# Output projection: the second half of the contraction by Strassen's scheme too

## The chip, the cores and the metric

The kernel runs on one core of a Trainium2 chip. The metric is device time in microseconds of one execution, the median of several runs. Engines: TensorE (PE; PEld is its weight load), VectorE (DVE), ScalarE (ACT), GpSimd (POOL) and SyncE (SP), which here only issues DMAs.

## The reference, cut to what matters

One inference step of an encoder layer for two request groups that share all weights: 256 prompt rows and 32 sample rows, model width 1024. All branch inputs come from one combined projection of x. Branch A is an mLSTM matrix memory with 4 heads of 256, branch B a sparse attention with 8 heads of 128. The end of the layer, where the change lies:

```python
branch_a = (hn * sigmoid(oa)) * silu(za)
branch_b = o_b * silu(zb)
mixed = sigmoid(ga) * (branch_a @ w_out_a) + sigmoid(gb) * (branch_b @ w_out_b)
y = layer_norm(DN_ALPHA * x + mixed @ w_o, ln_g, ln_b)   # w_o: 1024 x 1024
```

Beside y, the outputs are the new keys and values, the indexer keys, and the mLSTM states C, n and m of both groups.

## The kernel before, in words

**Precision.** All large products are made in three parts. An fp32 operand v is split into a high part (a copy to the rounded type fp32r, by ScalarE) and a low part (v minus the high part, by VectorE); the product is high x high + high x low + low x high. So each weight tile of 128 x 1024 costs one ScalarE pass (`unit_hi`, `split_hi`), one VectorE operation (`unit_lo`, `split_lo`) and three matmuls for each 128 x 128 block.

**Main loop.** `ORDER` lists 117 weight tiles; all but the last eight (the tiles of w_o) are steps of the main loop, a tile each, 24 matmuls of 288 columns in some 3.2 us. `load_plan` gives each tile a step at which its load is issued on SP's queue and one of eight staging buffers. From step `EARLY + 4` on only four of the eight buffers rotate; the other four hold the first four tiles of w_o. In step t, in this order: the loads, the low part of tile t+2, the evacuation of tile t-1, the high part of tile t+3, and the 24 matmuls of tile t, with the work listed for the step by `at` or `start` (`side`) in the middle of them. High and low parts lie in rings of four buffers each (`pair`). Each engine works strictly in the order in which its instructions are written.

**mixed.** The last 16 steps are the tiles of the gate ga and of w_out_a in turn. The evacuation of each w_out_a tile (L1012 to L1015) multiplies, adds onto branch B's part in `mB`, copies the sample columns and splits the result into `mxh`, `mxl`. `mixed` therefore stands with its features on the partitions, 8 blocks of 128 features.

**Output projection** (`finish`, L1159). The first 512 features are a 2 x 2 block product of token halves (128 rows) and halves of columns (512) done by Strassen's scheme in Winograd's form: seven products (`seventh`, L1079, of 6 matmuls of 512 columns each) in place of eight. It needs sums of token blocks s1 to s4 (`token_sums`, `token_halves`, one operation for all low parts, L1030) and differences of weight blocks t1 to t4 (`weight_sum`), made by VectorE during the main loop. The second 512 features are done plainly: four calls of `plain` (L1085), each of 4 x 3 matmuls. The four blocks of y lie in four PSUM banks y11, y12, y21, y22; VectorE adds them onto alpha * x, the residual, half a row at a time (`begun`, L1165; `added`, L1169). The bank y21 also serves as running total, from which VectorE reads between products. The sample rows are one plain product of 64 small matmuls (`sample_rows`, L1098).

**Layer norm.** For each block of 128 rows VectorE records statistics (L1172), aggregates them (`statistics`, L1151), GpSimd raises the variance to the power -0.5 (L1156), VectorE centres and multiplies by g (L1176), then scales and adds b (L1181). Row block 0 is finished while TensorE still works on row block 1. Row block 1's last half is written by the second DMA of L1185.

**States.** `state_prompt(h)` (L776) makes one head's C_prompt: 12 matmuls of 258 columns, two copies by ScalarE (L789), and DMAs (SP for heads 0 and 1, ScalarE's queue for 2 and 3). All four heads stand at the very end, behind the matmuls of y; head 3's copies and DMAs are written last.

Of the kernel before, what the change touches and what calls it, by code (L numbers as in the profile page):

```python
# [19 lines left out]
D = 1024  # L20
# [11 lines left out]
SEVEN = ("b11", "b21", "t2", "t1", "t3")  # L32
# [53 lines left out]
EARLY = WO - 20  # L86


def load_plan():
    slots, homes = defaultdict(list), {}  # L90
    for t in range(FIRST, EARLY + 9):
        slots[max(t - 9, FIRST)].append(t)
        homes[t] = (t - FIRST) % 8
    for i in range(4):
        slots[EARLY + i].append(WO + i)
        homes[WO + i] = (EARLY + 9 + i - FIRST) % 8
    rest = [*range(EARLY + 9, WO), *range(WO + 4, NT)]
# [14 lines left out]
def body(ctx, tc, a, o):  # L112
# [37 lines left out]
    def load_tile(t):  # L150
        if t >= NT or t in loaded:
            return
        loaded.add(t)
        stage[t] = sb(f"wst{t}", [128, KT * 128], tag=f"wst{HOMES[t]}")
        sp.dma_start(stage[t], a["w"][:, t - FIRST])
# [5 lines left out]
    def raw_unit(u):  # L161
        if u[0] == "t":
            return lazy["sums"][u]
        if u[0] == "b":
            return stage[POS["wo", ("b11", "b12", "b21", "b22").index(u)]]
        return stage[POS["wo", int(u[1])]]
# [7 lines left out]
    def unit_lo(u):  # L174
        wh, wl = split[u]
        dve.tensor_tensor(wl, raw_unit(u), wh.bitcast(F32), OP.subtract)

# [839 lines left out]
    def token_sums():  # L1017
        m = lazy["mB"]
        a11, a12 = m[:, 0:2, 0:128], m[:, 2:4, 0:128]
        a21, a22 = m[:, 0:2, 128:256], m[:, 2:4, 128:256]  # L1020
        s1, s2, s3, s4 = (lazy["sraw"][:, i].rearrange("p (k t) -> p k t", k=2) for i in range(4))
# [5 lines left out]
    def token_halves():  # L1027
        both = sb("sums", [128, 2, 4, 256], F32R, tag="kaT")
        act.copy(both[:, 0], lazy["sraw"])
        dve.tensor_tensor(both[:, 1], lazy["sraw"], both[:, 0].bitcast(F32), OP.subtract)  # L1030
        for i in range(4):
            lazy["s", i + 1] = tuple(both[:, e, i].rearrange("p (k t) -> p k t", k=2) for e in range(2))

    def weight_sum(name):
        if "sums" not in lazy:
            t = sb("t123", [128, 3, KT * 128], tag="a5")
            lazy["sums"] = {"t1": t[:, 0], "t2": t[:, 1], "t3": t[:, 2], "t4": sb("t4", [128, KT * 128], tag="wmat")}
        first, second = {"t1": ("b12", "b11"), "t2": ("b22", "t1"), "t3": ("b22", "b12"), "t4": ("b21", "t2")}[name]
        dve.tensor_tensor(lazy["sums"][name], raw_unit(first), raw_unit(second), OP.subtract)

    at(WO - 6, token_sums)
    at(WO - 4, token_halves)
    for i, n in enumerate(("t1", "t2", "t3", "t4")):
        at(EARLY + 5 + 2 * i, weight_sum, n)
# [34 lines left out]
    def seventh(p, x, u, first=False):  # L1079
        x = standing(x)  # L1080
# [4 lines left out]
    def plain(p, rows, column, first=False):  # L1085
        r = slice(128 * rows, 128 * rows + 128)
        for k in range(4, KT):
            group(p, (lazy["mxh"][:, k, r], lazy["mxl"][:, k, r]), split[f"w{k}"],
                  slice(512 * column, 512 * column + 512), first and k == 4, k == KT - 1)

    def sample_rows(p):
        for k in range(KT):
            for q in range(4):
                if k < 4:
                    w, c = stage[POS["wo", 2 * (k // 2) + q // 2]], 512 * (k % 2) + 256 * (q % 2)
                else:
                    w, c = stage[POS["wo", k]], 256 * q
# [33 lines left out]
    def load_tail():  # L1131
        lazy["xn"] = sb("xn", [128, 2, D], tag="vaT")
        sq = sb("sq", [128, 8, 256], tag="stC")
        lazy["zs"], lazy["gs"], lazy["bs"], lazy["xs"] = (sq[:, i] for i in range(4))
        lazy["sraw"] = sq[:, 4:8]
        lazy["bst"] = sb("bst", [128, 2, 2, 6], tag="sg", bufs=3)
        lazy["bss"] = sb("bss", [128, 4, 6])
        sp.dma_start(lazy["xn"], a["x_nat"][0:TP].rearrange("(b p) c -> p b c", p=128))
        sp.dma_start(lazy["xs"], ap_of(a["x_nat"], TP * D, [[256, 4], [D, TS], [1, 256]]))

    def load_affine():
        gb = sb("rest", [128, 2, D], tag="xhl")
        lazy["g"], lazy["b"] = gb[:, 0], gb[:, 1]
        sp.dma_start(gb, ap_of(a["ln_gb"], 0, [[0, 128], [D, 2], [1, D]]))
# [14 lines left out]
    def finish():  # L1159
        z, zs, bst, bss = lazy["xn"], lazy["zs"], lazy["bst"], lazy["bss"]  # L1160
        g, be = lazy["g"], lazy["b"]

        def begun(b, c, p):
            half = slice(512 * c, 512 * c + 512)
            dve.scalar_tensor_tensor(z[:, b, half], z[:, b, half], ALPHA, p, op0=OP.mult, op1=OP.add)  # L1165

        def added(b, c, p):
            half = slice(512 * c, 512 * c + 512)
            dve.tensor_tensor(z[:, b, half], z[:, b, half], p, OP.add)  # L1169

        def recorded(b, c):
            dve.bn_stats(bst[:, b, c], z[:, b, 512 * c:512 * c + 512])  # L1172

        def centred(b):
            mv, nr = statistics(b, slice(0, 128), bst[:, b].rearrange("p a b -> p (a b)"))
            dve.scalar_tensor_tensor(z[:, b], z[:, b], mv[:, 0:1], g, op0=OP.subtract, op1=OP.mult)  # L1176
            return nr[:, 1:2]

        def scaled(b, rs):
            for c in (slice(0, 512), slice(512, 1024)):  # L1180
                dve.scalar_tensor_tensor(z[:, b, c], z[:, b, c], rs, be[:, c], op0=OP.mult, op1=OP.add)  # L1181

        def put(c):
            c = slice(512 * c, 512 * c + 512)
            sp.dma_start(o["y"][128:256, c], z[:, 1, c])  # L1185

        own = sb("wown", [128, 2, KT * 128], F32R, tag="a1")
        spare = sb("spare", [128, 2, KT * 128], F32R, tag="a3")
        lazy["oc"] = sb("oc_all", [128, AH, 2, CROW], tag="a6")
        pool.memset(lazy["oc"][:, :, :, 257:], 0.0)  # L1190
        y11, y12, y21, y22 = (bank(f"yn{i}") for i in range(4))
        p = bank("yns")

        r = slice(96, 128)
        unit_lo("t2")
        evac(WO - 1, prev)
        seventh(y21, "a11", "b11", True)
        seventh(y11, "a12", "b21", True)
        unit_hi("t1")
        begun(0, 0, y21)  # L1200
        unit_lo("t1")
        sample_rows(p)
        unit_hi("t3")
        unit_lo("t3")
        unit_hi("w4")
        unit_lo("w4")
        unit_hi("w7", (own[:, 0], own[:, 1]))
        unit_lo("w7")
        seventh(y21, "s2", "t2")
        dve.scalar_tensor_tensor(zs, lazy["xs"], ALPHA, p[:, 0:256], op0=OP.mult, op1=OP.add)  # L1210
        dve.bn_stats(bss[:, 3], zs)
        begun(0, 1, y21)
        unit_hi("w5")
        unit_lo("w5")
        seventh(y12, "s1", "t1", True)
        begun(1, 1, y12)
        unit_hi("w6")
        unit_lo("w6")
        seventh(y21, "s3", "t3")
        unit_hi("b22")  # L1220
        unit_lo("b22")
        added(1, 1, y21)
        plain(y11, 0, 0)
        unit_hi("t4", (spare[:, 0], spare[:, 1]))
        unit_lo("t4")
        for q in range(3):
            dve.tensor_copy(bss[r, q], bss[32 * q:32 * q + 32, 3])
        mv, nr = statistics(2, r, bss[r].rearrange("p a b -> p (a b)"))
        for q in range(4):
            pool.tensor_copy(nr[32 * q:32 * q + 32, 0:1], mv[r, 0:1])  # L1230
        for q in range(3):
            pool.tensor_copy(nr[32 * q:32 * q + 32, 1:2], nr[r, 1:2])
        seventh(y12, "s4", "b22")
        plain(y12, 0, 1)
        added(0, 0, y11)
        recorded(0, 0)
# [3 lines left out]
        seventh(y21, "a22", "t4")  # L1240
        plain(y21, 1, 0)
        plain(y22, 1, 1, True)
        added(0, 1, y12)
        recorded(0, 1)
        rs = centred(0)
        scaled(0, rs)
        sp.dma_start(o["y"][0:128], z[:, 0])
        begun(1, 0, y21)
        recorded(1, 0)
        added(1, 1, y22)  # L1250
        recorded(1, 1)
# [73 lines left out]
def pack_weights(x, w_in, w_out_a, w_out_b, w_o):  # L1325
# [3 lines left out]
    for t, (n, j) in enumerate(ORDER):  # L1329
# [73 lines left out]
```

## Time and profile before

| what | us |
|---|---|
| median of 3 runs | 412.75 (411.69 to 412.89) |
| profiled execution | 411.89 |
| its span, first to last instruction | 410.2 |
| first wide matmul of the output projection | 375.9 |
| last matmul of y ends | 400.6 |
| issue of the last C_prompt DMA | 407.0 |

A line of a timeline gives start and length in us, engine, source line, operation, the tile written and the tiles read, and the shapes; in brackets stands the idle time of the engine ahead of it and what ended it. A line of the groups gives count, total busy time, mean duration of one in ns, and the idle time ahead. The tile names are those of the program without numbers: `wst` staging buffers, `wh` and `wl` high and low parts, `yn` the banks of y, `xn` the rows of y, `c` a state product.

### The profile page before, as it was taken

The numbers are of one execution on the slowest core, as the hardware profiler recorded it, in microseconds if no ns is written. First come the engines' busy times: TensorE is split into PE (matmuls) and PEld (weight loads), VectorE is DVE, ScalarE is ACT, GpSimd is POOL, SyncE is SP. The second block draws the span as 40 slices with busy tenths as digits, with TensorE's granted clock in tenths as the row PEclk, the third lists the DMA queues.
The fourth block names the chain that finished last, engine by engine and source line by source line (L and its number), as shares of the span: only waits on it lengthen the run. The fifth ranks groups of instructions, "written<-read, shape, count | busy, mean of one in ns | idle before, by whom it ended". The sixth has DMA issues, their size and how long they took to land.

```text
span 410.2 us, 8482 instructions
## 1 busy us (share of the span) xinstructions
PE 405.1 (99%) x3111; PEld 394.3 (96%) x3111; DVE 330.3 (81%) x674; ACT 220.6 (54%) x426; POOL 197.2 (48%) x448
## 2 busy tenths in 40 slices
PE   8999999999999999999999999999999999999996
PEld 6999999999999999999989999999999999998785
DVE  5878979997885878887968878988766677788985
ACT  5797563543765665576645545654444335474502
POOL 0210059993388657769800028547799846000031
PEclk9999999999999999999999999999999999999999
DMA  8987979787955655559943674454656557545005
GB/s 294 393 299 164 340 262 322 257 187 232 400 161 155 228 158 162 163 188 195 288 128 120 163 260 118 148 155 123 185 156 200 161 154 257 170 151 176 5 15 211
DMA packets 43151, 81.09 MB, mean 198 GB/s; under 512 B 20682, under 2 KB 25670, under 8 KB 42182
## 3 DMA queue, kind: packets, MB, share of 16 engines
q1 hardware_dynamic: 42390, 79.73, 62.2%
q10 hardware_dynamic: 720, 0.82, 0.6%
q8 instruction: 24, 0.39, 0.4%
q14 instruction: 17, 0.14, 0.1%
HBM read 73.38 MB, written 9.06 MB: 201 GB/s over the span
## 4 chain that ended last, share of the span: by engine, by line
PE 97%; DMA 1%; ACT 0%; SPq 0%; ACTq 0%; issue 0%; DVE 0%
PE pj L1063 27%; PE pj L1064 27%; PE pj L1062 27%; PE yn L1077 5%; PE pj L1126 1%; DMA wst_k<-in_first 1%; PE pj L1121 1%; PE yns L1098 1%; PE pj L1124 0%; PE ix L484 0%; PE al L640 0%; PE s L704 0%; PE av L673 0%; PE c L788 0%; PE c L786 0%; PE os L616 0%
## 5 line engine op out<-in xcount | busy, mean ns | idle before, releaser
L1063 PE MATMUL pj<-xhl,wh 128*128 128x288 f32 x704 | 207.7, 295 | 0.0
L1062 PE MATMUL pj<-xhl,wh 128*128 128x288 f32 x704 | 207.6, 295 | 0.0
L1064 PE MATMUL pj<-xhl,wl 128*128 128x288 f32 x704 | 207.5, 295 | 0.0
L194 DVE TENSOR_TENSOR wl<-wst,wh 128x1024 fp32r<-128x1024 f32 x104 | 129.8, 1249 | 13.8 <-ACT wh L186 13.5
L1062 PEld LDWEIGHTS pj<-xhl,wh 128*128 128x128 f32 x704 | 132.4, 188 | 0.6 <-issue 0.5
L1063 PEld LDWEIGHTS pj<-xhl,wh 128*128 128x128 f32 x704 | 132.4, 188 | 0.0
L1064 PEld LDWEIGHTS pj<-xhl,wl 128*128 128x128 f32 x704 | 132.3, 188 | 0.0
L186 ACT CAST wh<-wst 128x1024 fp32r<-128x1024 f32 x104 | 109.1, 1049 | 10.7 <-PE pj L1063 5.1
L141 POOL COPY pt<-bm 32x96 f32<-32x96 f32 x128 | 48.8, 381 | 19.9 <-DVE bm L656 10.7
L141 POOL COPY kaT<-kn 32x128 f32<-32x128 f32 x64 | 32.8, 513 | 5.1 <-DVE kn L754 2.5
L141 POOL COPY vn<-qaT 32x128 f32<-32x128 f32 x64 | 29.0, 453 | 2.6
L141 POOL COPY hn<-qaT 32x128 f32<-32x128 f32 x32 | 15.5, 485 | 12.1 <-DVE qaT L730 5.6
L141 POOL COPY hn<-ht 32x128 f32<-32x128 f32 x32 | 14.7, 459 | 9.3 <-DVE ht L730 8.0
L1062 PE MATMUL pj<-bah,wh 128*128 128x288 f32 x64 | 18.9, 296 | 0.0
L1063 PE MATMUL pj<-bal,wh 128*128 128x288 f32 x64 | 18.9, 296 | 0.0
L1064 PE MATMUL pj<-bah,wl 128*128 128x288 f32 x64 | 18.9, 296 | 0.0
L1062 PE MATMUL pj<-bbh,wh 128*128 128x288 f32 x64 | 18.9, 295 | 0.0
L1063 PE MATMUL pj<-bbl,wh 128*128 128x288 f32 x64 | 18.9, 295 | 0.0
L1064 PE MATMUL pj<-bbh,wl 128*128 128x288 f32 x64 | 18.8, 294 | 0.0
L999 ACT ACTIVATE sg<-pj 128x288 f32<-128x288 f32 x16 | 6.6, 410 | 22.1 <-PE pj L1064 22.1
L1014 POOL COPY mxs<-mB 128x32 f32<-128x32 f32 x8 | 1.9, 243 | 30.6 <-DVE mB L1013 30.5
L932 ACT CAST mxh<-mB 128x288 fp32r<-128x288 f32 x8 | 3.5, 433 | 22.2 <-DVE mB L1013 22.2
(510 smaller groups left out, 682.9 us busy)
## 6 DMA issues: line engine op xcount, KB each, us to landing
wst<-in_w SPq DMA_DIRECT2D x112, 512.0 KB, 4.1
wst_k<-in_first SPq DMA_DIRECT2D x5, 440.0 KB, 6.7
rscr<-rrow SPq DMA_DIRECT2D x2, 768.0 KB
out_k<-kbT SPq DMA_DIRECT2D x1, 1152.0 KB, 10.0
vrows<-vat SPq DMA_DIRECT2D x8, 144.0 KB, 1.8
stC<-in_state_C SPq DMA_DIRECT2D x1, 1028.0 KB
out_C_sample<-stC SPq DMA_DIRECT2D x1, 1028.0 KB
bm<-rscr SPq DMA_DIRECT2D x1, 1024.0 KB
```

Of the source, the lines that this page charges most:

```text
L141: pool.tensor_copy(out(quads[k], quads[i]), turned(quads[i], quads[k]))
L186: act.copy(split[t][0], stage[t])
L194: dve.tensor_tensor(wl, stage[t], wh.bitcast(F32), OP.subtract)
L932: act.copy(lazy[hi][:, j], v)
L999: act.activation(sg, q, AF.Sigmoid)
L1062: pe.matmul(p[:, :T], lhsT=wh[:, c], rhs=h[:, k], start=(k == 0), stop=False)
L1063: pe.matmul(p[:, :T], lhsT=wh[:, c], rhs=l[:, k], start=False, stop=False)
L1064: pe.matmul(p[:, :T], lhsT=wl[:, c], rhs=h[:, k], start=False, stop=(k == KT - 1))
L1077: pe.matmul(p, lhsT=l, rhs=r, start=first and i == 0, stop=last and i == 2, skip_group_check=True)
L1098: pe.matmul(p[32 * q:32 * q + 32, 0:256], lhsT=lazy["mxs"][:, k], rhs=w[:, c:c + 256], start=(k == 0), stop=(k == KT - 1))
L1121: pe.matmul(q, lhsT=part, rhs=xh[:, k, new], start=False, stop=(k == KT - 1))
L1126: pe.matmul(p[t][:, 0:2 * n].rearrange("p (a n) -> p a n", a=2), lhsT=part, rhs=xhl[:, :, k, new], start=False, stop=False)
```

## The change

1. *Products.* The second 512 features are done by Strassen's scheme as well, with weight blocks c11 to c22 beside b11 to b22 and differences u1 to u4 beside t1 to t4. `seventh` takes the token half from the first letter of the weight's name. Each product of the second half is accumulated into the same bank, right behind its fellow of the first half. So there are fourteen products of 6 matmuls; `plain` and the bank y22 go.
2. *Low parts by DMA.* `unit_summed` makes the low parts of b22 and c22 without VectorE: ScalarE writes the high part and, into the low part's buffer, the weight negated and rounded in the same way; a DMA on GpSimd's queue adds the unrounded weight onto it.
3. *Loads.* `EARLY` is WO - 25 instead of WO - 20. The other four tiles of w_o come in two loads of 1 MB at steps WO - 14 and WO - 10 (`load_two`); x's rows (z0, z1) and the affine rows g and b take the last places of the rotating staging buffers.
4. *Sums.* t1 to t3 are made at steps EARLY + 6 to EARLY + 8; u1 and u2 at WO - 4 and WO - 3; t4, u3 and u4 within `finish`, in place. The token sums of the second half are made for one pair of blocks at step WO - 1 (`pre_halves`, with the split of the first half's sums) and for the other within `finish`.
5. *Order in `finish`.* The products run a11 b11, a11 c11, a12 b21, a12 c21, then `state_prompt(0)`, the sample rows, then s2, s1, s3, s4 and a22, each with t or b22 and with u or c22. Heads 1 to 3 of the states stay at the end.
6. *Row block 0's layer norm.* ScalarE makes mean and squared deviation by two passes with accumulation over z0, VectorE centres z0 in place and multiplies by g, GpSimd scales the variance and takes the power, ScalarE multiplies by it, GpSimd adds b. Row block 1 keeps VectorE's way. Three small copies for the sample rows' statistics go from VectorE to ScalarE.

```diff
-SEVEN = ("b11", "b21", "t2", "t1", "t3")
+SEVEN = ("b11", "c11", "b21")
-EARLY = WO - 20
+EARLY = WO - 25
...
+    def unit_summed(u, home):
+        unit_hi(u, home)
+        act.mul(home[1], raw_unit(u), -1.0)
+        pool.dma_start(home[1].bitcast(F32), raw_unit(u), accum_op=OP.add)
...
+    def pre_halves():
+        halves_hi(0)
+        token_sums(1, slice(0, 1), lazy["sraw"][1])
+        halves_lo(0)
...
+    at(WO - 6, first_sums)
+    at(WO - 1, pre_halves)
+    for i, n in enumerate(("t1", "t2", "t3")):
+        at(EARLY + 6 + i, difference, n)
+    at(WO - 14, load_two, WO + 4, "vaT")
+    at(WO - 10, load_two, WO + 6, "stC")
+    at(WO - 4, difference, "u1")
+    at(WO - 3, difference, "u2")
```

The new `finish`, from its first product on:

```python
split_lo(WO + 2)
unit_hi("c21")
evac(WO - 1, prev)
...
seventh(y21, "a11", "b11", True)
seventh(y21, "a11", "c11")
seventh(y11, "a12", "b21", True)
unit_lo("c21")
seventh(y11, "a12", "c21")
halves_hi(1)
token_sums(1, slice(1, 2), lazy["sraw"][2])
unit_hi("t2")
halves_hi(2)
unit_lo("t2")
begun(0, 0, y21)
unit_summed("b22", own)
for i in (1, 2):
    halves_lo(i)
unit_hi("u2")
unit_lo("u2")
unit_hi("t1")
unit_lo("t1")
unit_hi("u1")
unit_lo("u1")
state_prompt(0)
sample_rows(p)
seventh(y21, "s2", "t2")
seventh(y21, "s2", "u2")
unit_summed("c22", spare)
...
difference("u3")
unit_hi("t3")
unit_lo("t3")
begun(0, 1, y21)
seventh(y12, "s1", "t1", True)
seventh(y12, "s1", "u1")
unit_hi("u3")
unit_lo("u3")
begun(1, 1, y12)
seventh(y21, "s3", "t3")
seventh(y21, "s3", "u3")
...
difference("t4")
unit_hi("t4")
difference("u4")
unit_hi("u4")
unit_lo("t4")
added(1, 1, y21)
unit_lo("u4")
seventh(y12, "s4", "b22")
seventh(y12, "s4", "c22")
added(0, 0, y11)
...
seventh(y21, "a22", "t4")
seventh(y21, "a22", "u4")
added(0, 1, y12)
act.activation(junk, z[0], AF.Identity, scale=-1.0 / D, accum_out=sums[:, 0:1])
act.activation(junk, z[0], AF.Square, bias=sums[:, 0:1], accum_out=sums[:, 1:2])
dve.bn_stats(bst[:, 1], z[1][:, col[1]])
dve.scalar_tensor_tensor(zs, zs, nr[:, 0:1], lazy["gs"], op0=OP.subtract, op1=OP.mult)
dve.scalar_tensor_tensor(z[0], z[0], sums[:, 0:1], g, op0=OP.add, op1=OP.mult)
pool.tensor_scalar(sums[:, 1:2], sums[:, 1:2], 1.0 / D, LN_EPS, op0=OP.mult, op1=OP.add)
pool.tensor_tensor(sums[:, 1:2], sums[:, 1:2], mhalf[:, 0:1], OP.pow)
act.mul(z[0], z[0], sums[:, 1:2])
...
pool.tensor_tensor(z[0], z[0], be, OP.add)
sp.dma_start(o["y"][0:128], z[0])
begun(1, 0, y21)
dve.bn_stats(bst[:, 0], z[1][:, col[0]])
mv, nr = statistics(1, slice(0, 128), bst.rearrange("p a b -> p (a b)"))
dve.scalar_tensor_tensor(z[1], z[1], mv[:, 0:1], g, op0=OP.subtract, op1=OP.mult)
for h in range(1, AH - 1):
    state_prompt(h)
for c in range(2):
    dve.scalar_tensor_tensor(z[1][:, col[c]], z[1][:, col[c]], nr[:, 1:2], be[:, col[c]], op0=OP.mult, op1=OP.add)
    sp.dma_start(o["y"][128:256, col[c]], z[1][:, col[c]])
state_prompt(AH - 1)
```

More of the change, by code (lines that the diff above doesn't have):

```diff
@@ L161, in raw_unit @@
     def raw_unit(u):
[L162 to L166, printed above, removed]
+        u = {"t4": "b21", "u3": "c12", "u4": "c21"}.get(u, u)
+        if u[0] in "tu":
+            return lazy[u]
+        return stage[WO + 4 * (u[0] == "c") + ("11", "12", "21", "22").index(u[1:])]
     def unit_hi(u, home=None):
@@ new lines, in halves_lo, with halves_of, difference @@
+    def halves_lo(i):
+        dve.tensor_tensor(halves_of(i, 1), lazy["sraw"][i], halves_of(i, 0).bitcast(F32), OP.subtract)
+    def halves_of(i, e):
+        v = lazy["halves"][:, int(i > 0), e]
+        return v if i == 0 else v[:, :, i - 1:i]
+    def pre_halves():
+        halves_hi(0)
+        token_sums(1, slice(0, 1), lazy["sraw"][1])
+        halves_lo(0)
+    def difference(name):
+        first, second = {"t1": ("b12", "b11"), "t2": ("b22", "t1"), "t3": ("b22", "b12"), "t4": ("b21", "t2"),
+                         "u1": ("c12", "c11"), "u2": ("c22", "u1"), "u3": ("c22", "c12"), "u4": ("c21", "u2")}[name]
+        if name == "t1":
+            t = sb("t123", [128, 3, KT * 128], tag="a5")
+            lazy.update(t1=t[:, 0], t2=t[:, 1], t3=t[:, 2])
+        if name == "u1":
+            t = sb("u12", [128, 2, KT * 128], tag="kaT")
+            lazy.update(u1=t[:, 0], u2=t[:, 1])
+        dve.tensor_tensor(raw_unit(name), raw_unit(first), raw_unit(second), OP.subtract)
@@ L1083, in seventh @@
             group(p, [v[:, k] for v in x], w, slice(512 * k, 512 * k + 512), first and k == 0, k == 1)
[L1085 to L1089, printed above, removed]
     def sample_rows(p):
@@ L1167, in added @@
         def added(b, c, p):
[L1168 to L1188, printed above, removed]
+            dve.tensor_tensor(z[b][:, col[c]], z[b][:, col[c]], p, OP.add)
@@ L1203, in finish @@
+        dve.bn_stats(bss[:, 3], zs)
+        difference("u3")
         unit_hi("t3")
         unit_lo("t3")
[L1205 to L1211, printed above, removed]
         begun(0, 1, y21)
-        unit_hi("w5")
-        unit_lo("w5")
         seventh(y12, "s1", "t1", True)
+        seventh(y12, "s1", "u1")
@@ L1231, in finish @@
[L1231 to L1236, printed above, removed]
+        seventh(y21, "s3", "u3")
+        for i in range(3):
+            act.copy(bss[r, i], bss[32 * i:32 * i + 32, 3])
+        difference("t4")
+        unit_hi("t4")
+        difference("u4")
+        unit_hi("u4")
+        unit_lo("t4")
+        added(1, 1, y21)
+        unit_lo("u4")
@@ new lines, in finish @@
+        seventh(y12, "s4", "b22")
+        seventh(y12, "s4", "c22")
+        added(0, 0, y11)
+        mv, nr = statistics(2, r, bss[r].rearrange("p a b -> p (a b)"))
+        for i in range(4):
+            pool.tensor_copy(nr[32 * i:32 * i + 32, 0:1], mv[r, 0:1])
+        for i in range(3):
+            pool.tensor_copy(nr[32 * i:32 * i + 32, 1:2], nr[r, 1:2])
+        seventh(y21, "a22", "t4")
+        seventh(y21, "a22", "u4")
+        added(0, 1, y12)
+        junk, sums = stage[WO + 4], sb("rowsum", [128, 2])
```

135 lines of the change are left out of this document (52 added, 83 removed).

## The prediction

> **What bounds the kernel now.** I read the page first (busy shares, the chain that ended last), then the chain and the busy time of each engine in the last 35 us, then the timelines of VectorE, ScalarE, GpSimd and the queues there.
>
> ```profile
> span 410.2 us, 8482 instructions
> PE 405.1 (99%) x3111; PEld 394.3 (96%) x3111; DVE 330.3 (81%) x674; ACT 220.6 (54%) x426; POOL 197.2 (48%) x448
> PE 97%; DMA 1%; ACT 0%; SPq 0%; ACTq 0%; issue 0%; DVE 0%
> ```
>
> TensorE is the bound: 97% of the chain. So the question for the output projection is first how many matmuls go, and then whether the others still hide. The chain there, and the busy time from its first matmul to its last (columns: PE, PEld, DVE, ACT, POOL):
>
> ```profile
> 375.91 2.79 PE yn L1077 x12
> 378.70 3.59 PE yns L1098 x64
> 382.30 18.34 PE yn L1077 x78
> 400.64 0.12 PE c L786
> ```
>
> ```profile
> 375.75:400.60 24.85, 24.85 (x158) 18.85 (x156) 22.57 (x36) 8.33 (x9) 3.80 (x11) 1.00 0.09 32
> ```
>
> The 90 wide matmuls come every 0.2325 to 0.235 us, without a gap; the full clock (1.00) is granted. But VectorE is busy 22.57 of the 24.85 us. It has hardly 2 us to give, and ScalarE has 16. The end:
>
> ```profile
> 400.89 0.67 DVE L1169 TENSOR_TENSOR xn<-xn,yn 128x512 f32<-128x512 f32 x1
> 401.60 0.69 DVE L1172 BATCH_NORM_STATS2 bst<-xn 128x6 f32<-128x512 f32 x1
> 402.32 0.21 DVE L1154 BATCH_NORM_AGGREGATE mv<-bst 128x2 f32<-128x12 f32 x1
> 402.57 0.15 DVE L1155 TENSOR_SCALAR mv<-mv 128x1 f32<-128x1 f32 x1
> 402.64 1.27 DVE L1176 SCALAR_TENSOR_TENSOR xn<-xn,mv,rest 128x1024 f32<-128x1024 f32 x1
> 404.36 1.41 DVE L1181 SCALAR_TENSOR_TENSOR xn<-xn,nr,rest 128x512 f32<-128x512 f32 x2 [0.45 <-POOL nr L1156]
> ```
>
> ```profile
> 405.14 0.99 SPq L1185 DMA_DIRECT2D out_y<-xn  x2
> ```
>
> ```profile
> 407.02 0.34 ACTq L791 DMA_DIRECT2D out_C_prompt<-oc_all  x1
> ```
>
> The last matmul of y ends at 400.64, VectorE takes the row block's second half over at 400.89 and the second half of y is issued about 405.80 (404.36 + 1.44). The last piece of C_prompt is issued at 407.02, and the span ends 3.18 us later. So y has 1.2 us of slack under the state products.
>
> **The change, part by part.** *Matmuls.* Before: seven Strassen products of 6 and 4 x 12 plain ones, 90. After: fourteen of 6, 84. Gain 6 x 0.235 = 1.4 us. The state products of head 0 (12 at 0.12 = 1.45 us) only move ahead of the sample rows; their write goes onto SP's queue, which is empty there. Without a stall the last y matmul ends where it did (400.64 - 1.41 + 1.45 = 400.7), and behind it stand 36 state matmuls instead of 48. That alone brings C_prompt 1.4 us forward and leaves y as the last, at 405.8: at best 1.2 us of gain.
>
> *Loads.* t1 to t3 and the loads of w_o move up to five steps earlier, two megabytes of w_o and the affine rows change places. I cost this at nothing: the queue waits for buffers, not for data, and data takes 4.1 us:
>
> ```profile
> SPq L155 <- DVE wl L194: 79.5, 28, 5.2
> wst<-in_w SPq DMA_DIRECT2D x112, 512.0 KB, 4.1
> ```
>
> If that cover failed, each late tile would stop TensorE by its lateness.
>
> *VectorE ahead of the products.* Where it stands before:
>
> ```profile
> 366.03 0.46 DVE L933 TENSOR_TENSOR mxl<-mB,mxh 128x288 fp32r<-128x288 f32 x1 [0.50 <-ACT mxh L932]
> 367.93 1.23 DVE L1030 TENSOR_TENSOR sums<-sq,sums 128x1024 fp32r<-128x1024 f32 x1 [1.44 <-ACT sums L1029]
> 371.34 0.45 DVE L1012 TENSOR_TENSOR sg<-pj,sg 128x288 f32<-128x288 f32 x1
> 373.75 1.23 DVE L176 TENSOR_TENSOR wl_b<-wst,wh_b 128x1024 fp32r<-128x1024 f32 x1 [0.50 <-ACT wh_b L172]
> 376.14 0.45 DVE L1012 TENSOR_TENSOR sg<-pj,sg 128x288 f32<-128x288 f32 x1
> 377.95 0.68 DVE L1165 SCALAR_TENSOR_TENSOR xn<-xn,yn 128x512 f32<-128x512 f32 x1
> 378.55 2.36 DVE L176 TENSOR_TENSOR wl_t<-t,wh_t 128x1024 fp32r<-128x1024 f32 x2
> ```
>
> A 128x1024 operation costs 1.14 when others follow (2.36 for two, less the 1.22 of the last). After 366.5 the changed kernel has four of them (u1, low of the last wa tile, u2, low of b11): 371.1, where it stood before (371.34), since the wait of 1.44 goes. 2.41 later (373.75 - 371.34) it starts low of c11; then four sums of one block each (about 1.0, from 0.42 for two blocks, below), low of the token sums and low of b21: 373.5 + 3 x 1.14 + 1.0 = 377.9. Before, the last wa tile was taken over at 376.14; now 1.75 later. With its 1.81 (377.95 - 376.14), low of c21 is ready at 380.9. TensorE wants it 19 matmuls in, at 375.9 + 4.4 = 380.3: a stall of about 0.7.
>
> *VectorE in the products.* These are the smaller prices:
>
> ```profile
> 359.26 0.42 DVE L1022 TENSOR_TENSOR sq<-mB 128x256 f32<-128x256 f32 x1
> 383.09 0.42 DVE L1210 SCALAR_TENSOR_TENSOR sq<-sq,yns 128x256 f32<-128x256 f32 x1
> 383.54 0.43 DVE L1211 BATCH_NORM_STATS2 bss<-sq 128x6 f32<-128x256 f32 x1
> ```
>
> From 380.85, in its order, up to the addition that completes row block 0: eleven operations of 1024 (low of t2, u2, t1, u1, t3, u3, t4, u4, differences u3, t4, u4) 12.5; five on half a row from PSUM at 0.60, 3.0; sums of the remaining blocks 1.05, their low parts 1.2, sample rows 0.85, their statistics 0.5; waits for ScalarE 0.7 (u2's high part stands behind b22's two passes). Sum 19.85: 400.7. TensorE has by then finished row block 0 (375.9 + 72 x 0.234 + 1.45 + 3.6 + 0.7 = 398.5). VectorE has become the bound, 2 us behind; the stall of 0.7 and TensorE's 1.4 no longer show.
>
> *The adding DMAs.* They take two low parts (2.3 us) off VectorE and cost ScalarE two passes more. ScalarE has the block sums at 381.9, then half a pass and b22's two: 384.4; then u2, t1, u1 (2.9), the two copies of head 0's state that now stand there (0.8) and c22's two: 390. TensorE wants them at 396 and 397.5, so 11 and 7.5 us are there. No row shows an adding DMA; nearest is the plain 512 KB load, 4.1. As it reads two operands I take up to twice that, 8: hidden, since VectorE is 2 us behind anyway. Behind each on GpSimd's queue stands only the sample rows' power, at 400. The Trainium skill (DMA: Bandwidth & Descriptors, Anatomy of one DMA) gives 2.0 us plus bytes at 436 GB/s for a DMA issued by GpSimd, by which it would be 3.2, estimated from that page, and the sum the same.
>
> *The end of row block 0* is what is new. Its statistics go to ScalarE (two passes with accumulation), the centring stays on VectorE and writes z0 in place, so it must wait until the second pass has read z0; ScalarE scales, GpSimd adds the shift. Queued behind the waiting centring on VectorE: all of row block 1. Queued behind the waiting addition on GpSimd: row block 1's power. Prices:
>
> ```profile
> 377.45 1.99 ACT L172 CAST wh_t<-t 128x1024 fp32r<-128x1024 f32 x2
> ```
>
> ```profile
> L772 ACT ACTIVATE kx<-kaT,gnat 128x256 fp32r<-128x256 f32 x8 | 3.6, 502 | 0.0
> L562 ACT CAST k6h<-kbT 128x256 fp32r<-128x256 f32 x1 | 0.4, 409 | 0.0
> L789 ACT COPY oc_all<-c 128x257 f32<-128x257 f32 x8 | 3.0, 377 | 15.3 <-PE c L788 15.3
> L650 ACT ACTIVATION_READ_ACCUMULATOR lg<-lg,st 128x1 f32 x16 | 3.1, 192 | 0.0
> L507 POOL TENSOR_TENSOR accs<-accs,srel 64x288 f32<-64x288 f32 x1 | 0.8, 812 | 26.3 <-ACT accs L506 26.3
> L510 POOL TENSOR_TENSOR accs<-accs,srel 32x288 f32<-32x288 f32 x1 | 1.4, 1408 | 6.2 <-ACT srel L509 6.2
> L299 POOL COPY bm<-bm 128x1024 f32<-128x1024 f32 x1 | 1.0, 1039 | 0.1
> ```
>
> ```profile
> 392.06 0.55 POOL L1156 TENSOR_TENSOR nr<-mv,mhalf 32x1 f32<-32x1 f32 x1 [14.71 <-DVE mv L1155]
> 402.80 1.53 POOL L1156 TENSOR_TENSOR nr<-mv,mhalf 128x1 f32<-128x1 f32 x1 [4.60 <-DVE mv L1155]
> ```
>
> A pass is 1.05 + 0.10 (scale or bias by row) + 0.19 (accumulator) = 1.34. GpSimd's add of 128x1024 isn't in the trace: at least the copy's 1.04, at most 1408 ns for 288 carried up, 4.5 (0.2 fixed); I take 812 ns carried up the same way, 2.4, as the 1408 ran beside a 1024 operation of VectorE. The power takes 0.55 alone, 1.53 beside VectorE's centring, ending 0.42 after it. The working:
> addition to 401.4; two passes to 404.15; centring (1.28) to 405.45; the power for row block 0 to 405.95; ScalarE's scaling (1.15) to 407.1; GpSimd's addition to 409.5; row block 1's power to 410.05; from there 1.44 to the second put, 411.5. Row block 1's own steps on VectorE (0.45 + 0.68 + 0.72 + 0.4 behind 405.45) are ready to centre at 407.7, in the middle of GpSimd's addition. If it isn't held, it is hidden; if it is held for the whole of it, put at 412.75. I take the middle, 412.1. C_prompt's six copies and two issues wait for ScalarE's scaling and take some 0.4 each, so its last piece is issued by 410.3. End: 412.1 + 3.3 = 415.4 against 410.2, **+5.2 us**.
>
> The Trainium skill (SBUF — State Buffer, Who interferes with whom) says that a Vector instruction with two SBUF inputs and a GpSimd one that reads SBUF block each other, the later until the earlier ends. The trace agrees where GpSimd is later (1.53 for 0.55); where VectorE is later no row of it is as long as this addition.
>
> The profiled execution took 411.89, 1.69 more than its span, so it would become 417.1; the median, 412.75, is 0.86 above that execution, so the forecast is 412.75 + 5.2 = **418.0**.
>
> **The rivals.** *Gain arrives* (other side): VectorE keeps pace with TensorE and row block 0's pieces don't hold row block 1. Then 1.2 us are won, 411.6. It decides if VectorE reaches row block 1's first half by about 401.4. For: six matmuls fewer are certain. Against: VectorE's 22.57 of 24.85 and its added operations. *Milder*: VectorE is on time (398.7 for 400.75) and GpSimd adds at the copy's rate. Then the centring waits alone count: passes to 402.1, centring 403.4, row block 1 centred by 407.3, second put 408.7, +1.8: 414.5; half of it, 416. *Held both ways*: the centring of row block 1 stands still for the whole addition, put 412.75: 418.6. *Adding DMA late*: landing over 9.7 us after its issue (7.5 + 2.2) moves the end one for one; at 15 it is 423.3. For: no row shows its rate. Against: the rings are nearly empty there (DMA share 0.09).
>
> **How the numbers follow.** Chances: forecast 0.42, held both ways 0.20, milder 0.20, DMA late 0.10, gain 0.08. Range 414.5 to 420.5: from VectorE on time (+1.8) to GpSimd's addition at its dearest (+2.1 on the forecast, and the hold). About 0.3%, 1.24 us, is what a measurement can tell here; the gain's 1.2 lies on that edge, so it is split: faster 0.04, same 0.05, slower 0.91.
>
> **What would show it.** Right: 84 matmuls into yn; a stall of TensorE under 1 us at the fourth product; VectorE without idle time from 377 to 400; the addition completing row block 0 at about 400.7 though its matmuls end at 398.5; VectorE idle over 1 us ahead of row block 0's centring, waiting for ScalarE; GpSimd's addition of 2 us or more ahead of row block 1's power; the last y issued after 411. Wrong: y issued before 408, VectorE idle among the products, or TensorE waiting for an adding DMA.

## The result, and the profile after

The changed kernel takes 416.99 us (median of 4 runs, 416.91 to 418.02), the kernel before, beside it on the same chip, 412.38 (411.69 to 412.89): ratio 1.0119, 95% interval 1.0095 to 1.0142. Slower by 1.2%, at 416.99 where 418.0 was forecast: the median rose by 4.6 us. The profiled execution took 416.95 us, its span 415.2. From its page, the span, the busy shares and the chain that ended last by engine:

```profile
span 415.2 us, 8508 instructions
PE 404.1 (97%) x3105; PEld 393.6 (95%) x3105; DVE 337.3 (81%) x679; ACT 229.9 (55%) x441; POOL 203.7 (49%) x452
PE 90%; DVE 5%; ACT 2%; POOL 1%; issue 1%; POOLq 0%; DVEq 0%; ACTq 0%
```

TensorE has six instructions fewer and is still busy 97% of the span, yet its share of the chain has gone from 97% to 90%. The chain itself, from the addition that completes row block 0 to the last y, has no matmul in it (columns: start, length in us, what):

```profile
400.24 0.70 DVE wstz L1192
400.96 1.16 ACT two L1263 x2
402.14 1.25 ACT two L1264 x2
...
403.57 1.19 POOL rowsum L1268
...
404.84 0.69 POOL rowsum L1269
405.56 1.16 ACT wstz L1270
...
406.78 2.34 POOL wstz L1273
409.13 1.51 POOLq L1411
...
410.66 0.75 DVE wstz L1282
```

It walks through row block 0's layer norm, engine by engine, then through GpSimd's queue to row block 1's power and scaling. The queue's piece at 409.13 bears the number of the line that encloses the whole program (L1411); the timeline of GpSimd below shows the power of L1179 there. The timeline of VectorE shows what row block 1 waits for (in brackets the idle time ahead):

```profile
377.46 0.45 DVE L1026 TENSOR_TENSOR sg<-pj,sg 128x288 f32<-128x288 f32 x1
...
384.96 1.23 DVE L185 TENSOR_TENSOR wl_u<-u,wh_u 128x1024 fp32r<-128x1024 f32 x1 [0.59 <-ACT wh_u L181]
...
400.24 0.69 DVE L1192 TENSOR_TENSOR wstz<-wstz,yn 128x512 f32<-128x512 f32 x1
...
403.42 1.29 DVE L1267 SCALAR_TENSOR_TENSOR wstz<-wstz,rowsum,wstg 128x1024 f32<-128x1024 f32 x1 [1.06 <-ACT two L1264]
...
406.78 3.43 DVE L1278 SCALAR_TENSOR_TENSOR wstz<-wstz,mv,wstg 128x1024 f32<-128x1024 f32 x1
410.66 1.41 DVE L1282 SCALAR_TENSOR_TENSOR wstz<-wstz,nr,wstb 128x512 f32<-128x512 f32 x2 [0.45 <-POOL nr L1179]
```

The centring of row block 1 (L1278) lasts 3.43 us; the same operation on row block 0 (L1267) lasts 1.29. No idle time is booked ahead of it; the operation itself is long. It starts together with GpSimd's addition, as the timeline of GpSimd shows:

```profile
403.57 1.19 POOL L1268 TENSOR_SCALAR rowsum<-rowsum 128x1 f32<-128x1 f32 x1 [0.94 <-ACT two L1264]
...
406.78 2.34 POOL L1273 TENSOR_TENSOR wstz<-wstz,wstb 128x1024 f32<-128x1024 f32 x1 [1.26 <-ACT wstz L1270]
409.09 1.54 POOL L1179 TENSOR_TENSOR nr<-mv,mhalf 128x1 f32<-128x1 f32 x1
```

The whole 2.34 us of the addition are in it, and 1.09 of its own behind. Busy time of the engines, clock, DMA share and GB/s over the output projection and over the last stretch (columns as before):

```profile
375.40:401.00 25.60, 25.04 (x162) 19.16 (x161) 24.25 (x34) 15.47 (x22) 2.86 (x6) 1.00 0.25 53
...
410.00:414.00 4.00, 0.00 (x0) 0.00 (x0) 1.62 (x3) 0.00 (x0) 0.62 (x1) 0.57 0.97 367
```

In the products VectorE is busy 24.25 of 25.60 us (before, 22.57 of 24.85). TensorE stalls once, for the low part of c21, and the last two halves of y are issued by SP at 411.44:

```profile
375.40 0.40 PE L1115 MATMUL yn<-wh_b,mxh 128*128 128x512 f32 x1
...
380.55 0.50 PE L1115 MATMUL yn<-wl_c,mxh 128*128 128x512 f32 x1 [0.56 <-DVE wl_c L185]
```

```profile
411.44 0.99 SPq L1283 DMA_DIRECT2D out_y<-wstz  x2
```

The two adding DMAs, in the list of DMA issues (size, time from issue to landing), leave no wait of TensorE behind them:

```profile
wown<-wst POOLq DMA_DIRECT2D x1, 512.0 KB, 5.3
spare<-two POOLq DMA_DIRECT2D x1, 512.0 KB, 4.6
```

### The profile page after: what moved, and what is told of

Read it like the earlier page. It is cut to its first block, busy times and chain, and to the rows that moved or that the text cites. A ratio compares the mean times of both kernels' runs of the same rounds, so it can differ in the third digit from the quotient of the medians.

```text
span 415.2 us, 8508 instructions
## 1 busy us (share of the span) xinstructions
PE 404.1 (97%) x3105; PEld 393.6 (95%) x3105; DVE 337.3 (81%) x679; ACT 229.9 (55%) x441; POOL 203.7 (49%) x452
## 4 chain that ended last, share of the span: by engine, by line
PE 90%; DVE 5%; ACT 2%; POOL 1%; issue 1%; POOLq 0%; DVEq 0%; ACTq 0%
PE pj L1101 27%; PE pj L1100 26%; PE pj L1102 26%; PE pj L1155 1%; DVE wl_u L185 1%; PE pj L1150 1%; DVE wl_t L185 1%; POOL wstz L1273 1%; PE pj L1148 1%; PE ix L498 0%; DVE wstz L1192 0%; PE warm_p L218 0%; PE pj L1153 0%; PE al L654 0%; PE s L718 0%
## 5 line engine op out<-in xcount | busy, mean ns | idle before, releaser
L141 POOL COPY kaT<-kn 32x128 f32<-32x128 f32 x64 | 34.0, 531 | 4.4 <-DVE kn L768 1.8
```

Source lines behind the costliest of these rows:

```text
L141: pool.tensor_copy(out(quads[k], quads[i]), turned(quads[i], quads[k]))
```

## The experiments

**How they are compared.** The profiles begin the main loop up to 1.4 us apart, ahead of anything that was edited. The first full tile's first matmul, in the timeline of the changed kernel and then of the eleventh experiment:

```profile
17.79 0.31 PE L1100 MATMUL pj<-xhl,wh 128*128 128x288 f32 x1
```

```profile
18.83 0.30 PE L1100 MATMUL pj<-xhl,wh 128*128 128x288 f32 x1
```

From there to the first wide matmul of the output projection both take 357.61 us (375.40 and 376.44). So F, the start of the first wide matmul, is the zero for every comparison of traces below; P is the start of the issue of the last two halves of y (the two issues take 0.99 us together in the changed kernel, 1.76 in e8 and 1.61 in e9, so that P flatters these two). The medians carry the start as well, and stand beside; each ratio is to runs of the kernel before on the same chip (medians 411.95 to 412.40).

| run | median us | ratio to before (95%) | F | P - F | end - F |
|---|---|---|---|---|---|
| before | 412.38 | | 375.75 | 29.39 | 34.45 |
| changed kernel | 416.99 | 1.0119 (1.0095 to 1.0142) | 375.40 | 36.04 | 39.80 |
| e1 low by VectorE | 419.82 | 1.0180 (1.0164 to 1.0195) | 376.03 | 37.60 | 42.47 |
| e2 six matmuls more | 417.25 | 1.0118 (1.0103 to 1.0133) | 375.37 | 36.03 | 39.83 |
| e3 no shift | 415.93 | 1.0081 (1.0064 to 1.0098) | 375.62 | 33.86 | 38.78 |
| e4 row block 0 on VectorE | 417.42 | 1.0119 (1.0104 to 1.0134) | 376.13 | 35.38 | 39.57 |
| e5 before + new layer norm | 413.31 | 1.0027 (1.0016 to 1.0037) | 375.66 | 30.13 | 35.64 |
| e6 reordered | 419.08 | 1.0151 (1.0113 to 1.0189) | 376.32 | 34.49 | 42.28 |
| e7 less written | 416.19 | 1.0092 (1.0076 to 1.0107) | 376.24 | 33.90 | 37.76 |
| e8 write only (one run) | 417.15 | | 375.74 | 34.64 | 39.66 |
| e9 differences by DMA | 423.27 | 1.0265 (1.0240 to 1.0289) | 376.33 | 39.66 | 45.97 |
| e10 same, statistics by ScalarE | 422.21 | 1.0237 (1.0214 to 1.0260) | 376.18 | 38.43 | 44.12 |
| e11 no differences | 415.91 | 1.0087 (1.0072 to 1.0103) | 376.44 | 34.25 | 38.06 |
| e12 e11 and e4 together | 415.94 | 1.0084 (1.0067 to 1.0102) | 376.68 | 33.59 | 38.22 |

**Is VectorE the bound of the products? e1, e2.** The theory was the prediction's: VectorE runs behind TensorE, then row block 0's layer norm holds row block 1. The first rival: TensorE is still the bound. e1 gives VectorE two operations more, e2 gives TensorE six wide matmuls more.

```diff
-        act.mul(home[1], raw_unit(u), -1.0)
-        pool.dma_start(home[1].bitcast(F32), raw_unit(u), accum_op=OP.add)
+        unit_lo(u)
```

> The changed kernel, but the low parts of b22 and c22 are made by VectorE again (no adding DMA, no negating pass on ScalarE). Theory (VectorE bounds the output projection from the last steps of the main loop on): two more operations of 1.14 us, less the 0.59 us that VectorE waited for ScalarE behind the negating pass: the addition that completes row block 0 moves from 400.2 to about 401.9 and the end by +1.7 us, 418.7. Rival (TensorE bounds it still, VectorE has room): 417.0, unchanged.

```diff
+        for k in range(2):
+            group(extra, [v[:, k] for v in standing("a22", 0)], own, slice(512 * k, 512 * k + 512), k == 0, k == 1)
         seventh(y21, "a22", "t4")
```

> The changed kernel with six more 512-column matmuls into an unused bank ahead of the last two products, so that TensorE has as many as before the change. Theory (VectorE is the bound; it takes the last product over only at 405.0, while TensorE has it at about 401): no change, 417.0, and y's last product ends 1.4 us later in the trace. Rival (TensorE is the bound): +1.4 us, 418.4.

e1, the timeline of VectorE and of SP's queue: the addition that completes row block 0, and the last put.

```profile
402.44 0.69 DVE L1191 TENSOR_TENSOR wstz<-wstz,yn 128x512 f32<-128x512 f32 x1
```

```profile
413.63 0.99 SPq L1282 DMA_DIRECT2D out_y<-wstz  x2
```

Both stand 1.56 us later behind F than in the changed kernel (402.44 - 376.03 = 26.41 against 400.24 - 375.40 = 24.84; P 37.60 against 36.04): of VectorE's two operations (2.3 us) two thirds reach the put, 1.56 where 1.7 was expected. The median rose by 2.83. Between the two profiles the span rises by 3.3 us: 1.56 up to P, 1.1 behind it (the end came 4.9 us behind P and not 3.8) and 0.6 ahead of F. e2 changed nothing: P 36.03, end 39.83. So 1.4 us more of TensorE's work ahead of the last two products do not show, and VectorE's do. The products of row block 0 stand ahead of e2's matmuls, so e2 says nothing of them; there the timeline of the changed kernel does: TensorE has them behind it when it starts the next product at 398.14, and VectorE comes to the completing addition only at 400.24. The rival fell.

**What does GpSimd's addition do? e3, e8.** e3 leaves the addition of b to rows 0 to 127 out; e8 puts two fills of the same rows in its place, which write and do not read.

```diff
-        pool.tensor_tensor(z[0], z[0], be, OP.add)
+        pool.memset(z[0], 0.0)      # e8 only
+        pool.memset(z[0], 1.0)      # e8 only
```

> The changed kernel without GpSimd's addition of ln_b to the first 128 rows of y, which is left out. Theory (that addition holds the centring of row block 1 for its whole length, and row block 1's power behind it on its queue): the centring takes 1.28 us in place of 3.43, the power ends 0.4 us behind it, the last y is issued about 2.1 us earlier: 414.9. Rival (the addition is only beside it, and the power alone waits for it on the queue): the centring keeps its length and the end moves by under 0.5 us, 416.7.

> The changed kernel with GpSimd's addition of ln_b to the first 128 rows replaced by two fills of that tile, so those rows are not computed. A fill only writes. Theory (VectorE's centring, which reads two operands from SBUF, is held because GpSimd reads SBUF): the centring beside the fills takes its 1.3 us. Rival (any GpSimd instruction on SBUF holds it): it takes about as long as the fills, 2.4 us or more.

e8, the timelines of VectorE and of GpSimd:

```profile
407.11 1.28 DVE L1279 SCALAR_TENSOR_TENSOR wstz<-wstz,mv,wstg 128x1024 f32<-128x1024 f32 x1
```

```profile
407.10 0.95 POOL L1273 MEMSET wstz<- 128x1024 f32 x1 [1.24 <-ACT wstz L1270]
408.10 0.95 POOL L1274 MEMSET wstz<- 128x1024 f32 x1
```

With a fill beside it the centring takes 1.28 us; with the addition beside it, 3.43. So it is not GpSimd's being busy, nor its writing of row block 0, that holds VectorE: what the addition does and the fills do not is to read. The time of e8, one execution, did not fall all the same (417.15). In e3 the centring takes 1.27 and P moves by 2.18, the expected 2.1. The end moved by 1.02 only: behind P stand 4.9 us in place of 3.8. By P the theory held, by the time it got half of what it expected.

**Where did the other half go? e7.** e3, and three of the four C_prompt heads are computed but not written, 816 KB less.

> The kernel without GpSimd's addition (ln_b left out for the first 128 rows), and in addition C_prompt of heads 1 to 3 is computed but not written (0.8 MB less). Theory (without the addition the last y was issued 2.2 us earlier, but the end came only 1.0 us earlier since all outputs were then written in one rush at a DMA share of 1.0): with less to write the end follows the issue by about 3.1 us again: 1.1 us below the kernel without the addition, 414.8. Rival (something else sets the end): no change, 415.9.

P stayed (33.90), the end behind F came 1.02 earlier, but the median did not fall (416.19 after 415.93). The median does not decide here: the main loop begins at 18.63 in e7's profile and at 18.00 in e3's, and that takes 0.63 of the 1.02. The DMA engines do (the last two columns are their share and the GB/s). First the changed kernel, its rush of writes and its last 1.25 us:

```profile
408.75:413.75 5.00, 0.00 (x0) 0.00 (x0) 2.87 (x3) 0.38 (x1) 1.88 (x2) 0.68 0.97 366
413.95:415.20 1.25, 0.00 (x0) 0.00 (x0) 0.00 (x0) 0.00 (x0) 0.00 (x0) 0.50 0.00 0
```

Then e3, e8 and e7:

```profile
407.75:412.75 5.00, 0.00 (x0) 0.00 (x0) 1.92 (x3) 0.99 (x3) 0.92 (x1) 0.76 1.01 381
```

```profile
409.00:414.00 5.00, 0.00 (x0) 0.00 (x0) 1.41 (x2) 0.37 (x1) 0.57 (x2) 0.61 0.99 374
```

```profile
408.50:412.50 4.00, 0.00 (x0) 0.00 (x0) 1.82 (x3) 0.70 (x3) 0.82 (x1) 0.54 0.69 267
```

In the changed kernel, e3 and e8 the outputs fill the DMA engines for 5 us, and the span ends 1.45, 1.65 and 1.4 us behind these. So in e3 and e8 the end follows the writes, not the last put. Behind F the 5 us begin at 33.35 in the changed kernel, at 32.13 in e3 and at 33.26 in e8, and the end moves likewise: by 1.02 in e3 and by 0.14 in e8, though P moved by 2.18 and 1.40. What e3 has and e8 has not is the early write of row block 0: its put is issued at 409.15 in the changed kernel, 406.93 in e3, 409.08 in e8. In e7 the engines are no longer full (0.69). So the hold itself is worth little at the end, as far as one execution of e8 shows it. What stays open is the stretch from P to the end in e1, 4.9 us.

**The layer norm alone. e4, e5.** e4 has row block 0's layer norm back on VectorE within the changed kernel; e5 puts the new one into the kernel before.

```diff
-        act.activation(junk, z[0], AF.Identity, scale=-1.0 / D, accum_out=sums[:, 0:1])
-        act.activation(junk, z[0], AF.Square, bias=sums[:, 0:1], accum_out=sums[:, 1:2])
...
-        pool.tensor_tensor(z[0], z[0], be, OP.add)
+        dve.bn_stats(bs0[:, 1], z[0][:, col[1]])
+        mv0, nr0 = statistics(0, slice(0, 128), bs0.rearrange("p a b -> p (a b)"))
...
+            dve.scalar_tensor_tensor(z[0][:, col[c]], z[0][:, col[c]], nr0[:, 1:2], be[:, col[c]], op0=OP.mult, op1=OP.add)
```

> The changed kernel with row block 0's layer norm on VectorE as before the change; all else as changed. Theory (VectorE is the bound and 2 us behind; spreading the layer norm saves it work but makes it wait): the waits and the hold go (1.06 and 2.15 us), 1.4 of statistics and 1.4 of scaling come back onto VectorE: -0.6 us, 416.4. Rival (the spread layer norm is the whole loss): the time of the kernel before less its gain, 411.5.

> The kernel before, with only the new layer norm of row block 0 (two passes and the scaling on ScalarE, centring on VectorE, power and addition on GpSimd). Theory (the new layer norm costs by holding row block 1, and does so only where row block 0 ends shortly ahead of it): here row block 0 ends 7 us ahead of row block 1's last product, so passes end at 398, the centring at 399.3, GpSimd's addition at 403.5; it still holds row block 1's centring by some 0.9 us, against 1.2 us of slack of y under the state products: +0.2 us, 412.6. Rival (the new layer norm is dear wherever it stands): the hold and the waits in full, +3 us, 415.4.

e4: P moved by 0.66, as expected, the time not measurably (the main loop of its profile begins 0.73 later). VectorE's own operations for row block 0 cost about what ScalarE and GpSimd cost by waits and hold. e5, the timeline of VectorE:

```profile
397.84 1.28 DVE L1247 SCALAR_TENSOR_TENSOR xn<-xn,rowsum,rest 128x1024 f32<-128x1024 f32 x1 [2.50 <-ACT t L1246]
...
402.37 2.19 DVE L1176 SCALAR_TENSOR_TENSOR xn<-xn,mv,rest 128x1024 f32<-128x1024 f32 x1
```

The same kind of wait (2.50) and of hold (2.19 for 1.28) are there; P moves by 0.74 and the time by 1.1 us, ratio 1.0027: more than the 0.2 expected, well under the 3 of the rival. The 0.74 are about the 0.66 of e4, so the new layer norm costs the put much the same in either kernel, and the theory's "only where row block 0 ends shortly ahead" is not borne out. What differs between the kernels is when row block 0 becomes complete. In the kernel before:

```profile
394.74 0.68 DVE L1169 TENSOR_TENSOR xn<-xn,yn 128x512 f32<-128x512 f32 x1
```

That is 18.99 us behind F, 6.15 ahead of row block 1's last addition (400.89), and from there VectorE works off both layer norms one behind the other, 10.40 us to P. In the changed kernel it is 24.84 behind F and 11.20 to P. So of the 6.65 us by which P moved, 5.85 lie ahead of the completing addition and 0.80 behind it.

**The parts of the loss. e11, e12.** Both leave VectorE's last three differences out; e12 has e4's layer norm as well.

```diff
-        difference("u3")
-        difference("t4")
-        difference("u4")
```

> Leaves out part of the computation: u3, t4 and u4 are not formed (c12, b21 and c21 are used in their place), so VectorE does three operations of 1.14 us less between the first products and row block 0's last addition; all else as in the changed kernel. If VectorE's backlog of about 2 us behind TensorE is one part of the loss and the way row block 0's layer norm holds row block 1 the other: the addition that completes row block 0 comes about 1.8 to 2.2 us earlier (about 22.8 us after the first wide matmul instead of 24.84, now when TensorE allows it), the second put 34.6 after it instead of 36.7, GpSimd's addition holds the centring of row block 1 as before; time about 415, still slower than before. If the backlog were the whole loss: 412 or less. If it were not a loss (TensorE or a DMA as late): 417 as the changed kernel.

> Leaves out the same part (u3, t4 and u4 not formed) and has row block 0's layer norm wholly on VectorE, as in the run of that part alone. If both are parts of the loss and what then remains is that two layer norms follow each other on VectorE at the end: row block 0's last addition at about 22.9 us after the first wide matmul, second put at about 33.6 instead of 36.07 in the run of that part alone, time about 414 to 415, still slower than before (30.05). If GpSimd's hold were the main loss once the backlog is gone: second put below 32, time 412 or less.

e11, the timeline of VectorE (the addition completing row block 0, row block 1's centring) and of SP's queue; then e12's VectorE from that addition to the first step of row block 1:

```profile
399.48 0.69 DVE L1192 TENSOR_TENSOR wstz<-wstz,yn 128x512 f32<-128x512 f32 x1
...
406.02 3.44 DVE L1275 SCALAR_TENSOR_TENSOR wstz<-wstz,mv,wstg 128x1024 f32<-128x1024 f32 x1
```

```profile
410.69 1.00 SPq L1280 DMA_DIRECT2D out_y<-wstz  x2
```

```profile
400.32 0.67 DVE L1192 TENSOR_TENSOR wstz<-wstz,yn 128x512 f32<-128x512 f32 x1
...
406.01 0.68 DVE L1189 SCALAR_TENSOR_TENSOR wstz<-wstz,yn 128x512 f32<-128x512 f32 x1
```

In e11 the addition stands 23.04 behind F (24.84 in the changed kernel) and P 1.79 earlier, the end 1.74: the backlog. The hold is as long as ever (3.44). Between e11 and e12 P moves by another 0.66, as it did between the changed kernel and e4. What remains, 33.59 against 29.39, is 4.2 us: in e12 the completing addition stands 23.64 behind F, still 4.65 later than before, 5.69 us of VectorE's work for row block 0 and the sample rows stand between the two rows above, and TensorE's last wide matmul has started at 401.93. The new order explains most of it: TensorE starts the product behind row block 0's last at 22.74 behind F in the changed kernel (398.14), at 19.16 before (394.91). Of these 3.6 us, 1.4 are 72 wide matmuls in place of 66 up to there, 1.45 head 0's state products, which now stand ahead of the sample rows, and 0.56 the stall at c21. That is read from the traces; no run puts head 0's state products back or keeps the old order. The times agree less sharply: 415.9 for both where 415 and 414 to 415 were expected, still slower than before, as expected; the main loops of their profiles begin 1.04 and 1.26 later than the changed kernel's. Neither the backlog nor the hold alone is the whole loss.

**Can it be mended? e6, e9, e10.** e6 completes row block 0 one product earlier (s4 ahead of s3) and takes two low parts more off VectorE by adding DMAs, with row block 0's layer norm back on VectorE. e9 has the same aim another way: it makes the three differences by ScalarE (negates) and an adding DMA each, with the sample rows moved ahead, the last product in a bank of its own and the same layer norm on VectorE; e10 is e9 with row block 0's statistics on ScalarE.

```diff
+        unit_summed("t3", pair("_t3"))      # e6
+        unit_summed("u3", pair("_u3"))      # e6
...
+    def negated_plus(u, plus):              # e9, e10
+        act.mul(raw_unit(u), raw_unit(u), -1.0)
+        pool.dma_start(raw_unit(u), raw_unit(plus), accum_op=OP.add)
```

> The changed kernel with the products in the order s1, s2, s4, s3, a22 (row block 0 complete two products earlier), the low parts of t3 and u3 by adding DMAs too, the sample rows' normalization late, and row block 0's layer norm on VectorE as before the change. Theory (VectorE's backlog and the way in which row block 0's layer norm holds row block 1 are the loss): VectorE loses two operations (2.3 us), the hold (2.2) and the wait for ScalarE (1.1) and takes back 2.2 us of statistics and scaling; the last y is issued 3 to 3.5 us earlier and the time falls by about 3 us, 414.0. TensorE stalls about 2 us on the two new low parts, hidden. Rival (TensorE's stalls count): 416.0 or more. Not under the kernel before in either.

> The changed kernel, reordered: products s2, s1, s4, s3, a22 (row block 0 complete one product earlier), the sample rows ahead of the product of c21, the differences u3, t4 and u4 no longer by VectorE (3.4 us) but by ScalarE (negates) and an adding DMA each, the last product in a bank of its own, row block 0's layer norm wholly by VectorE. If VectorE's backlog and two layer norms at the very end are the whole loss: no stall of TensorE, VectorE ready for row block 1's last addition within 1.5 us of TensorE's last wide matmul, second put about 30.5 to 31.5 us after the first wide matmul, where the kernel before stands at 30.05; time 412 to 413.5. Rival, adding DMAs behind each other land late as in the earlier reordering (up to 6.4 us each): TensorE waits for t4 and u4, 415 or more.

> As the run beside it, but the statistics of row block 0 by two ScalarE passes with accumulation in place of VectorE's (1.8 us less on VectorE), no operation of GpSimd on whole rows. If VectorE's work is still the bound: second put 1 to 1.8 us earlier than in the run beside it; time 411.5 to 412.5. If TensorE (or an adding DMA it waits for) is the bound there: the same time as the run beside it.

All three miss, on the rival's side. e10 has P 1.23 earlier than e9, as expected of an engine relieved, but both stand over 2 us behind the changed kernel. In e6 the completing addition comes 4 us earlier (397.13, 20.81 behind F), but TensorE now waits for adding DMAs (its timeline), and VectorE for TensorE. Its four executions took 417.6, 417.7 and twice 420.5. In the profiled one (420.5) the sample rows are put last, at 411.89, and the span ends 7.8 us behind P:

```profile
398.20 0.50 PE L1115 MATMUL yn<-wl_t,halves 128*128 128x512 f32 x1 [1.13 <-DMA wl_t<-t]
400.77 0.50 PE L1115 MATMUL yn<-wl_u,halves 128*128 128x512 f32 x1 [0.91 <-DMA wl_u<-two]
```

e10, its DMA issues in order (time from issue to landing last), its timeline of TensorE, and its stretches (columns as before: the clock and the DMA share stand ahead of the GB/s):

```profile
wown<-wst POOLq DMA_DIRECT2D x1, 512.0 KB, 4.7
two<-two POOLq DMA_DIRECT2D x1, 512.0 KB, 5.7
spare<-two POOLq DMA_DIRECT2D x1, 512.0 KB, 6.2
t<-wst POOLq DMA_DIRECT2D x1, 512.0 KB, 7.3
u<-two POOLq DMA_DIRECT2D x1, 512.0 KB, 7.9
```

```profile
396.99 2.93 PE L1119 MATMUL yn<-wown,halves 128*128 128x512 f32 x6 [4.32 <-DVE wstz L1193]
```

```profile
388.00:392.00 4.00, 4.00 (x19) 3.31 (x18) 1.99 (x3) 3.93 (x9) 1.73 (x2) 1.00 1.03 194
...
396.00:400.00 4.00, 3.01 (x7) 2.43 (x8) 1.47 (x4) 1.05 (x1) 1.83 (x8) 0.50 0.76 156
```

Two bounds took VectorE's place in e10, and a third shows. First ScalarE: busy 3.93 of 4.00 us, since each negation is a pass more; the high part of t3 came late, the addition behind it on VectorE too, and TensorE stood for 4.32 us. Then the clock: after that stand it is granted at 0.50, and six matmuls take 2.93 us in place of 1.4. Last the adding DMAs: the engines are full (share 1.03) at 194 GB/s, where the plain writes of the changed kernel's end fill them (0.97) at 367. ScalarE waits 3.60 us for t4's there; TensorE, at its lower clock, has no idle time behind the 4.32. No version made here is faster than the kernel before.

## Why the prediction was right, step by step

*Matmuls, loads.* 84 came out, the loads cost nothing (357.61 us from the first full tile to F; the kernel before takes 357.62, from 18.13 to 375.75), the stall at c21 was 0.56 for 0.7. As forecast, TensorE's 1.4 us bring nothing; e2 bears it out for the last two products.

*VectorE behind.* The last w_out_a tile was taken over at 377.46 (377.9 forecast), the wait for u2's high part was 0.59 (0.7), the completing addition at 400.24 (400.7). Set against F it is 24.84 and 24.8. The mechanism is shown by e1 and e11, and e11 gives its size: 1.8 us, where 2 were forecast.

*Adding DMAs.* 5.3 and 4.6 us, between the plain load's 4.1 and the bound of 8, and hidden. The estimate of 3.2 from the Trainium skill (DMA: Bandwidth & Descriptors, Anatomy of one DMA) was too low for DMAs that add; five of them in a row took up to 7.9 in e10 and 8.2 in e9. The rival "adding DMA late" did not come here, but it is what e6 ran into, where TensorE waited 1.13 and 0.91 us for two of them.

*Row block 0's end.* Here two sizes were wrong and cancelled, by luck. ScalarE's two passes took 1.18 and 1.28, not 1.34 each, and started earlier; but GpSimd's first small operation (L1268), which the sum had not priced apart, took 1.19 beside VectorE's centring, so the addition started at 406.78 (407.1 forecast) and took 2.34 (2.4). Then came the step that was mis-sized: "I take the middle" between no hold and a hold for the whole addition. Measured, it is the whole, 3.43 us for 1.28. The rival "held both ways" had the mechanism right. The last put of y came at about 412.1 (411.44 and two thirds of 0.99), as forecast, since what came before was some 0.4 earlier than in the sum. Set against F it came 36.70 behind, where the forecast has 36.35.

The hold of row block 1's centring agrees with what the Trainium skill (SBUF — State Buffer, Who interferes with whom) states: a Vector instruction with two SBUF inputs contends with a GpSimd one that reads SBUF, not with one that only writes it. e3 (1.27 without the addition) and e8 (1.28 beside a fill) bear out both halves.

*The end.* The sum let the end follow the last put by 3.3 us, and it came 3.1 behind it. But the last put does not rule alone: the writes fill the DMA engines (0.97) until the last 1.25 us, and in e8, without the hold, the end came only 0.14 earlier. The prediction had no term for that; that the put and the writes end together here is luck too. From e7, whose last put is followed by the last write some 1.7 us later (410.80 to 412.5), the changed kernel's put alone would end the writes at an estimated 413.8, and they end by 413.95.

*The sum.* +5.2 forecast for the span, +5.0 measured (415.2 for 410.2), 5.35 from F on. Of P's 6.65 us against F, e11 and e12 give 1.8 to the backlog, 0.7 to ScalarE's and GpSimd's share in row block 0, and leave 4.2. These go with the order in `finish`: TensorE reaches the end of row block 0 3.6 us later, and both layer norms move with it. This part is argued from the traces, not shown by a run. Of the 6.65, 5.35 reach the end; in the kernel before C_prompt was issued last, 1.2 us behind y.

*Still open.* Gains of 2.2 us (e3) and 2.45 us (e12) at the put became 1.0 and 1.6 at the end. For e3 the writes account for it; for e12, and for the longer stretch in e1, no run settles it.

## What to carry to other kernels

Before trading matmuls for sums, look at the busy share of the engine that makes the sums in that stage alone, and at where the last outputs become complete: six matmuls were worth nothing where VectorE had 2 of 25 us to give, and completing row block 0 some 3 us of TensorE's time ahead of row block 1, instead of 6, moved two layer norms, which VectorE works off one behind the other, toward the end. An operation moved to GpSimd to relieve VectorE held VectorE for its whole length here (2.34 us), since it read SBUF beside an operation of two SBUF inputs. Before a put is made earlier, look whether the writes already fill the DMA engines: then the end does not follow it. And an experiment that relieves one engine should be costed on the next two, as e9 and e10 were not.

## What the runs showed of the hardware

- VectorE's 128x1024 operation with two SBUF inputs took 3.43 us when it started together with GpSimd's addition of 2.34, 1.28 beside a fill. Small operations of GpSimd are stretched the other way: 1.19 and 1.54 us for 128x1, beside such an operation, the power 0.56 in e8 and the multiply-and-add 0.19 in e10 without one.
- DMAs that add 512 KB from SBUF to SBUF landed after 4.6 to 5.3 us in the changed kernel, the two of them 5.5 us apart, and after 4.7 to 8.2 in e9 and e10, five behind each other, where they filled all DMA engines at 194 GB/s.
- The outputs at the end of the changed kernel filled the DMA engines for 5 us (share 0.97) at 366 GB/s; the engines were empty for the last 1.25 us.
- After a stand of 4.32 us TensorE's clock was granted at 0.50, and a wide matmul took 0.49 us in place of 0.234 (2.93 / 6).
